# Where an expert's overflow block stands: in front of its products instead of between them

## The chip, the cores and the metric

The kernel runs on one core of a Trainium2 chip. Its engines work side by side and wait for one another through semaphores: PE (TensorE, the matrix products), DVE (VectorE), ACT (ScalarE), POOL (GpSimd), and SP (SyncE), which here issues all DMA transfers. The metric is the device time of one execution in microseconds; below, a time without another word is the median of the runs shown.

## What is computed

One layer of a diffusion backbone over 256 tokens of width 1024: a token mixer (Fourier mixing, a state space scan, gates and an output projection), and then a mixture of experts, 4 of 32 for each token. Only the last part is touched by the change, apart from some preparation for it. In the reference it is

```python
logits = (tok @ w_router + b_router).astype(jnp.float32)
top_logit, top_idx = lax.top_k(logits, TOP_K)
top_w = jax.nn.softmax(top_logit, axis=-1)
...
def expert_block(args):
    xe, e = args
    gu = xe @ w_gate_up[e] + b_gate_up[e]
    gate = jnp.minimum(gu[:, :D_FF], SWIGLU_LIMIT)
    up = jnp.clip(gu[:, D_FF:], -SWIGLU_LIMIT, SWIGLU_LIMIT)
    act = (up + 1.0) * gate * jax.nn.sigmoid(SWIGLU_ALPHA * gate)
    return act @ w_down[e] + b_down[e]
...
x = x + g2 * moe_ffn(h2, ...)
return rmsnorm(x, final_norm_w)
```

A token's four results are weighted with `top_w` and added up; `g2` is a row that depends on the conditioning vector. The weights of one expert are 12 MB in float32.

## The kernel before

**The weights.** `expert_chunk` loads an expert's weights in twelve copies of 1 MB (128 partitions of 2048 floats): numbers 0 to 7 are the rows of gate and up, 8 to 11 those of down. All copies of all experts, 384, go through SP's one queue in that order. They land in a ring of 19 tiles of 1 MB (`RING`); one of these holds router data at first, so that 18 copies are there before the first tile has to be used again. From then on a copy is issued when the tile of the copy 19 before it has been released, that is, when the last instruction that reads it is past. Copy 7 of expert e+1 takes the tile of copy 0 of expert e.

**One expert.** Each expert has 64 slots for tokens (`CAP`). For an expert `e` the loop at L1444 to L1493 writes, in the order of the program: the one-hot matrices for a later pair of experts, or in odd experts the weights for scattering (`weights_T`: four DVE instructions make `woh`, PE turns it over, ACT copies it to `woT`); `gate_up` (L1277, 64 products on copies 0 to 7, then four short products with `bgu` that add the bias); `gate_act` and `up_act` (DVE and ACT); `gather` (48 short products that fetch the tokens of a later pair into `xe`); in even experts `scatter_pair`, which adds the results of the pair before to `acc`; `act_T` (PE turns the activations, DVE copies them to `aT`); `overflow`; `down` (L1323, 32 products on copies 8 to 11); and `gated`, where DVE multiplies with `g2b`.

**The overflow block.** `overflow` is a branch on the number of the expert's tokens, which all engines take. Only where it is over 64 does `block32` run: it gathers 32 more tokens, makes their gate and up products from the same copies 0 to 7 (in two passes, on the banks `gu`), their down products from copies 8 to 11, and scatters them. With these inputs it runs in experts 9, 20 and 24, once each. Since the block may read copies 0 to 7, their tiles are released only when PE is past the branch. A hint for the branch's target (`mark_branch_hint_location`) is given to PE in the first products of `gate_up`.

**The order.** In this part the program's order is each engine's order (`manual_schedule`). Waits on what another engine made ahead of a branch are waits for that engine to be past the branch.

**The bias of down** is added for all experts at once, in expert 1 (`down_bias`, L1243): PE turns the routing weights, multiplies them with `b_down` (`bd`, held in `xe[1]`), and DVE multiplies with `g2r` and adds to `acc`. Since `bd` occupies `xe[1]`, both gathers of the second pair follow in expert 1.

**Ahead of the experts** `bias_parts` (L484) splits the gate and up biases into three bfloat16 parts in `bgu`, so that short products with a selecting matrix `sel` add them; it is called four times while the gates of the mixer are computed. `routing_weights` makes the softmax weights on DVE and ACT.

Of the kernel before, what the change touches and what calls it, by code (L numbers as in the profile page):

```python
# [22 lines left out]
NE = 32  # L23
# [38 lines left out]
def build(tc, A, out):  # L62
# [37 lines left out]
    bgu = const.tile([96, 2048], BF16, name="bgu")  # L100
    sel = const.tile([96, 32], BF16, name="sel")
# [384 lines left out]
    def bias_parts(q):  # L486
        b0, b1 = t2("bg", (96, 512)), t2("bgh", (96, 512), BF16)
        sl = slice(q * 512, (q + 1) * 512)
        for i in range(3):
            nc.sync.dma_start(b0[32 * i:32 * i + 32], A["b_gate_up"][0, :, sl])  # L490
        S.activation(b1, b0, AF.Copy)
        V.tensor_sub(b0, b0, b1)
        V.tensor_copy(bgu[0:32, sl], b1[0:32])
        V.tensor_copy(bgu[32:64, sl], b0[32:64])
        V.tensor_copy(b1[64:96], b0[64:96])
        V.tensor_sub(bgu[64:96, sl], b0[64:96], b1[64:96])
# [339 lines left out]
    for ch in range(2):  # L836
        for q in range(2):
            bias_parts(2 * ch + q)
# [152 lines left out]
    g2r = few[:, 0:1024]  # L991
# [7 lines left out]
    wT = few[0:32, 1024:1280].rearrange("p (t c) -> p t c", t=2)  # L999
# [5 lines left out]
    def ahead():  # L1005
# [12 lines left out]
        yield rows_bc(g2r, modd[3072:4096])  # L1018
# [107 lines left out]
    ohx = keepA.tile([128, 2, 64], BF16, name="ohx")  # L1126
    woh, woT = (keepA.tile([128, 2, 128], F32, name=n) for n in ("woh", "woT"))
# [50 lines left out]
    bd = xe[1][0:32].rearrange("p a b -> p (a b)")  # L1178
# [8 lines left out]
    def gather_tokens(ps, o, k, tb, start, stop, **kw):  # L1187
        for part in range(3):
            T.matmul(ps, h2p[tb][part][:, k * 128:(k + 1) * 128], o[:, tb, :], start=start and part == 0,
                     stop=stop and part == 2, **kw)  # L1190
# [12 lines left out]

    def first_gather(k4, tb):
        for k in range(4):
            gather_tokens(xp[k4][:, k, :], oh[0], k4 * 4 + k, tb, tb == 0 and k == 0, tb == 1,
                          skip_group_check=True)
# [35 lines left out]
    def down_bias():  # L1243

        tp = bank("t", 3, shape=(128, 2, 128))
        for tb in range(2):
            T.transpose(tp[0:32, tb, :], wn[:, tb, :], ident)
        V.tensor_copy(wT, tp[0:32])
        tmp = ga
        for tb in range(2):  # L1250
            for n in range(2):
                ps = bank("sc", 2)
                T.matmul(ps, wT[:, tb, :], bd[:, n * 512:(n + 1) * 512], start=True, stop=True)
# [295 lines left out]
```

## Time and profile before

| | us |
|---|---|
| time, median of 3 runs (1599.68 to 1601.88) | 1599.94 |
| the profiled execution | 1596.67 |
| its span, from the first to the last instruction | 1594.9 |
| first product of expert 0, after the span's start | 582.91 |
| PE busy | 1432.5 (90%) |
| DVE busy | 660.2 (41%) |
| moved by DMA | 511.75 MB |

The experts take the time from 583 us to the end. The profile cuts the span into 40 slices and gives the busy share of the engines, the granted clock of PE and the DMA rate in each. It groups the instructions by line, with their busy time and what they waited for; a timeline gives single instructions, with the time that their engine sat idle before them and, behind an arrow, what ended that idle time. `PEq L1425` as such an end means that PE's sequencer had got past the branch at L1425, `DVEq L1425` that DVE's had. PEld stands for PE's loading of weights, which goes on beside its products.

### The profile page before, as it was taken

The page shows a single profiled execution, that of the slowest core. Times are in us where ns is not written, and L with a number is a line of the kernel's source. Part 1 is how long each engine was busy: PE and PEld are TensorE (multiplying, and loading weights), DVE is VectorE, ACT ScalarE, POOL GpSimd, SP SyncE. Part 2 cuts the span into 40 slices and gives each one's busy share as a digit, 9 for nine tenths or more (in the row PEclk, how much of TensorE's full clock was granted, in tenths as well). Part 3 has the DMA queues.
Part 4 walks back from the last instruction along what each step waited for, and adds up shares of the span by engine and source line. Part 5 has one row for each costly group of instructions (what it writes and reads, how often), then busy time and mean ns, then how long its engine had stood idle before and what let it go on. Part 6 is the DMA issues. An engine that isn't in the chain of part 4 may idle for free. (4 is left out here: it accounts for less than half of the span.)

```text
span 1594.9 us, 21869 instructions
## 1 busy us (share of the span) xinstructions
PE 1432.5 (90%) x8684; PEld 806.0 (51%) x8684; DVE 660.2 (41%) x1158; ACT 304.1 (19%) x635; POOL 200.9 (13%) x165
## 2 busy tenths in 40 slices
PE   6998988889999988998988889989888989899897
PEld 4887766678899753433333333433334334343332
DVE  5776887885575743212222222212213123121222
ACT  3446354444555420000000000000000000000001
POOL 0155143332460410000000000000000000000000
PEclk8999999999999978999999999999989999999999
DMA  9625244578769757999999899999997999699993
GB/s 290 215 76 192 87 125 158 151 231 278 274 235 339 268 211 316 384 418 418 419 418 418 351 418 418 418 419 418 418 419 299 418 418 417 257 418 418 418 418 154
DMA packets 121636, 511.75 MB, mean 321 GB/s; under 512 B 13800, under 2 KB 30928, under 8 KB 72448
## 3 DMA queue, kind: packets, MB, share of 16 engines
q1 hardware_dynamic: 121472, 509.56, 81.8%
q8 instruction: 103, 1.69, 0.4%
q14 instruction: 61, 0.50, 0.1%
HBM read 508.33 MB, written 1.20 MB: 319 GB/s over the span
## 5 line engine op out<-in xcount | busy, mean ns | idle before, releaser
L1277 PE MATMUL ps_gu<-wexp,xe 128*64 128x512 f32 x2048 | 462.2, 607 | 6.3 <-DMA wexp<-in_w_gate_up 6.3
L1277 PEld LDWEIGHTS ps_gu<-wexp,xe 128*64 128x64 f32 x2048 | 157.1, 140 | 294.9 <-issue 269.9
L1323 PE MATMUL ps_dn<-wexp,aT 128*64 128x512 f32 x1024 | 234.2, 610 | 32.5 <-DVEq L1425 21.3
L1292 DVE TENSOR_SCALAR ga<-ps_gu 128x512 f32<-128x512 f32 x32 | 22.1, 691 | 437.7 <-issue 405.6
L1323 PEld LDWEIGHTS ps_dn<-wexp,aT 128*64 128x64 f32 x1024 | 85.6, 140 | 169.8 <-issue 120.3
L343 PE MATMUL ps_mm<-hh,wh 128*128 128x256 f32 (+1 forms) x496 | 166.8, 336 | 2.3 <-DVE cv L472 2.3
L345 PE MATMUL ps_mm<-hh,wl 128*128 128x256 f32 (+1 forms) x496 | 163.1, 329 | 0.0
L344 PE MATMUL ps_mm<-hl,wh 128*128 128x256 f32 (+1 forms) x496 | 162.6, 328 | 0.0
L1293 ACT ACTIVATE ga<-ga 128x512 f32<-128x512 f32 x32 | 20.2, 631 | 660.5 <-DVE ga L1292 660.5
L1328 DVE TENSOR_TENSOR yp<-ps_dn,g2b 64x512 f32<-64x512 f32 x60 | 41.3, 689 | 231.1 <-PE ps_dn L1323 230.6
L336 POOL TENSOR_TENSOR wl<-wraw,wh 128x512 fp32r<-128x512 f32 x78 | 105.0, 1349 | 218.7 <-ACT wh L333 164.0
L1502 POOL TENSOR_TENSOR ssq<-ssq,mhalf 128x1 f32<-128x1 f32 x2 | 1.1, 550 | 1013.2 <-DVE ssq L1501 1013.2
L343 PEld LDWEIGHTS ps_mm<-hh,wh 128*128 128x128 f32 x496 | 95.3, 192 | 23.8 <-issue 7.7
L345 PEld LDWEIGHTS ps_mm<-hh,wl 128*128 128x128 f32 x496 | 95.5, 193 | 10.0 <-issue 2.2
L344 PEld LDWEIGHTS ps_mm<-hl,wh 128*128 128x128 f32 x496 | 95.4, 192 | 8.2 <-issue 1.2
L333 ACT ACTIVATE wh<-wraw 128x512 fp32r<-128x512 f32 x132 | 81.1, 627 | 86.3 <-PE ps_mm L344 71.6
L472 DVE SCALAR_TENSOR_TENSOR cv<-ps_mm,par,cv 128x508 f32<-128x508 f32 (+3 forms) x116 | 80.8, 697 | 5.0 <-ACT cv L466 3.2
L336 DVE TENSOR_TENSOR wl<-wraw,wh 128x512 fp32r<-128x512 f32 x54 | 49.8, 924 | 36.3 <-ACT wh L333 35.5
L1334 DVE TENSOR_TENSOR acc<-acc,ps_sc 128x512 f32<-128x512 f32 x76 | 51.5, 685 | 19.0 <-PE ps_sc L1332 17.0
L1332 PE MATMUL ps_sc<-yp,woT 128*128 128x512 f32 x120 | 57.4, 601 | 0.0
L706 ACT ACTIVATE ab<-ab,nacs 128x128 f32<-128x128 f32 x128 | 42.1, 390 | 51.9 <-POOL ab L703 51.7
L1310 ACT ACTIVATE woT<-ps_t 128x256 f32<-128x256 f32 x15 | 5.8, 384 | 237.2 <-PE ps_t L1309 237.2
(373 smaller groups left out, 1809.5 us busy)
## 6 DMA issues: line engine op xcount, KB each, us to landing
wexp<-in_w_gate_up SPq DMA_DIRECT2D x256, 1024.0 KB, 19.9
wexp<-in_w_down SPq DMA_DIRECT2D x127, 1024.0 KB, 19.9
wraw<-in_w_in SPq DMA_DIRECT2D x32, 1024.0 KB, 5.0
wmod<-in_w_mod SPq DMA_DIRECT2D x64, 256.0 KB, 5.3
wmod<-in_w_mod SPq DMA_DIRECT2D x16, 512.0 KB, 8.3
ab<-ad SPq DMA_DIRECT2D x32, 256.0 KB, 3.7
eb<-ad SPq DMA_DIRECT2D x32, 256.0 KB
wssd<-in_w_ssd_out SPq DMA_DIRECT2D x8, 1024.0 KB, 8.6
```

The costliest lines, as they stand in the source:

```text
L333: S.activation(shp, w, AF.Copy)
L336: e.tensor_sub(low.rearrange("p (k n) -> p k n", n=128), w, shp.bitcast(F32))
L343: T.matmul(ps[:, :N], hi, hh[k][:, :N], start=k == 0 and start, stop=False, **kw)
L344: T.matmul(ps[:, :N], hi, hl[k][:, :N], start=False, stop=False, **kw)
L345: T.matmul(ps[:, :N], low, hh[k][:, :N], start=False, stop=k == 7, **kw)
L472: V.scalar_tensor_tensor(yv[:, :, a], pv[:, :, b], convw(k, blk), yv[:, :, a], op0=OP.mult, op1=OP.add)
L706: S.activation(ab[:, h, :], ab[:, h, :], AF.Exp, bias=nacs[:, c, j0 + h:j0 + h + 1])
L1277: mm = T.matmul(ps[half][h * 64:h * 64 + 64, :], x[:, k, :], w[k][:, half, h * 512:(h + 1) * 512], start=k == 0, stop=False)
L1323: T.matmul(pd[n * 64:n * 64 + 64, :], aT[:, j, h * 64:h * 64 + 64], w[8 + h * 2 + j // 2][:, j % 2, n * 512:(n + 1) * 512], start=i == 0, ...
L1328: V.tensor_mul(y, p[n * 64:n * 64 + 64, :], g2b[n * 64:n * 64 + 64])
L1332: T.matmul(p, lhsT, rhs, start=True, stop=True)
L1334: V.tensor_add(av, av, p)
```

## The change

`overflow(e, n_e, w)` is called ahead of the expert's `gate_up`. Its wide products use the banks `t` instead of `gu`. Outside the branch, copies 0 to 7 are now read last by `gate_up`. The hint moves: that for expert e+1 is given after the second wide product of `down` of expert e, and that for expert 0 in `first_gather`.

`down` begins with two short products that add the down bias from `bdn`, which two more calls of `bias_parts` make, scaled by 1.702; `down_bias`, `g2r`, `bd` and `wT` go, and with them the copy of `g2r` and that of `b_down` in float32. The gathers of the second pair are spread over experts 0 and 1 as for all others.

`weights_T` is parted: `weights_of` (DVE) stays ahead of `gate_up`, `weights_turned` (PE and ACT) goes behind `gather`. `act_T` writes its result over the expert's own tokens in `xe` instead of to `aT`.

```diff
     def bias_parts(q):
...
+        if q > 3:
+            sl, src, dst = slice((q - 4) * 512, (q - 3) * 512), A["b_down"], bdn
         for i in range(3):
-            nc.sync.dma_start(b0[32 * i:32 * i + 32], A["b_gate_up"][0, :, sl])
+            nc.sync.dma_start(b0[32 * i:32 * i + 32], src[0, :, sl])
+        if q > 3:
+            V.tensor_scalar_mul(b0, b0, ALPHA)
...
-        for q in range(2):
-            bias_parts(2 * ch + q)
+        for q in range(3):
+            bias_parts(3 * ch + q)
...
-    def down_bias():
...
+    def weights_turned(t):
         tp = bank("t", 3, shape=(128, 2, 128))
         for tb in range(2):
             T.transpose(tp[:, tb, :], woh[:, tb], ident)
         S.activation(t, tp, AF.Copy)
...
-    def down(w, aT):
+    def down(e, w, aT, hint=None):
         pd = bank("dn", 1)
+        for n in range(2):
+            T.matmul(pd[n * 64:n * 64 + 64, :], sel[:, e:e + 1].to_broadcast([96, 64]), bdn[:, half(n)],
+                     start=True, stop=False)
...
-        p = bank(*GU[0], shape=(128, 256))
+        p = bank("t", 3, shape=(128, 256))
...
+    def hint_after(mm, hint):
+        with tc.issue_after(mm.ins):
+            tc.mark_branch_hint_location(hint, "LikelyTaken", [ET.PE])
...
         n_e = nc.values_load(cnt[0:1, e:e + 1], min_val=0, max_val=256)
-
-        if e == NE - 2:
-            wo2 = [xe[1 - p2][:, 2 * i:2 * i + 2, :] for i in range(2)]
-            for i in range(2):
-                weights_T(wo2[i], first, (e + i,))
-        elif e % 2 and not last:
-            weights_T(woT, first, (e - 1, e))
-        elif e + 2 < NE:
+        overflow(e, n_e, w)
+
+        if e >= NE - 2:
+            wo2.append(xe[0][:, 2 * (e % 2):2 * (e % 2) + 2, :])
+            weights_of(first, (e,))
+        elif e % 2:
+            weights_of(first, (e - 1, e))
+        else:
             one_hot(oh[1 - p2], (e + 2, e + 3), 0)
-        pg, pu = gate_up(e, xs, w, last_between if last else None, f"spill{e}")
+        pg, pu = gate_up(e, xs, w, last_between if last else None)
         gate_act(pg)
         up_act(pu)
-        if last:
-            GU[0] = ("t", 3)
-        if e == 1:
-            down_bias()
-        if e > 1 and e // 2 * 2 + 2 < NE:
+        if e // 2 * 2 + 2 < NE:
             gather(xe[1 - p2], oh[1 - p2], e % 2)
+        if e >= NE - 2 or e % 2:
+            weights_turned(wo2[-1] if e >= NE - 2 else woT)
         if e and e % 2 == 0:
             scatter_pair(0)
-        act_T(aT)
+        act_T(xs)
         if e and e % 2 == 0:
             scatter_pair(1)
...
-        if e == 1:
-            for k4 in range(2):
-                gather(xe[1], oh[1], k4)
-        overflow(e, n_e, w)
-        pd = down(w, aT)
+        pd = down(e, w, xs, None if last else f"spill{e + 1}")
```

How this moves PE's instructions is seen at three places. The first is the end of the branch of expert 17 on PE, before the change. The unconditional branch closes the block, `ps_dn` are the products of `down`, `ps_gu` those of `gate_up` of expert 18, and a DMAHW is the landing of a copy:

```order
L1425 UNCONDITIONAL_BRANCH [waits PE_49]
L1323 MATMUL ps_dn<-wexp,aT 64x512 [waits DMAHW5_49,DVE_49,PE_49]
L1323 MATMUL ps_dn<-wexp,aT 64x512 x3
L1323 MATMUL ps_dn<-wexp,aT 64x512 [waits DMAHW6_49]
L1323 MATMUL ps_dn<-wexp,aT 64x512 x3
L1323 MATMUL ps_dn<-wexp,aT 64x512 [waits DMAHW7_49]
L1323 MATMUL ps_dn<-wexp,aT 64x512 x3
L1323 MATMUL ps_dn<-wexp,aT 64x512 [waits DMAHW0_49]
L1323 MATMUL ps_dn<-wexp,aT 64x512 x3
L1457 TENSOR_LOAD cnt
L1277 MATMUL ps_gu<-wexp,xe_6123 64x512 [waits DMAHW1_49]
L1277 MATMUL ps_gu<-wexp,xe_6123 64x512 x3
```

After the change the branch of expert 17 stands between the last products of expert 16's `down` (here L1326) and the first of `gate_up` of expert 17 (here L1274); the rows of the block itself are left out:

```order
L1326 MATMUL ps_dn<-wexp,xe_6143 64x512 [waits DMAHW0_49]
L1326 MATMUL ps_dn<-wexp,xe_6143 64x512 x3
L1463 TENSOR_LOAD cnt
L1431 COMPARE_AND_BRANCH
...
L1433 UNCONDITIONAL_BRANCH [waits PE_49]
L1431 UNCONDITIONAL_BRANCH [waits PE_49]
L1274 MATMUL ps_gu<-wexp,xe_6143 64x512 [waits DMAHW1_49,PE_49]
L1274 MATMUL ps_gu<-wexp,xe_6143 64x512
```

The first wide product behind the branch waited for DVE and waits now, in all experts but expert 0, for a copy and for PE's own work alone; the load of the count and the comparison now follow `down` directly.

The second place is the start of expert 0 on PE. Before, its first products follow the load of the count, and the branch comes later:

```order
L1457 TENSOR_LOAD cnt [waits DVE_49]
L1277 MATMUL ps_gu<-wexp,xe_6122 64x512 [waits DMAHW0_49,DVE_49]
L1277 MATMUL ps_gu<-wexp,xe_6122 64x512
L1277 MATMUL ps_gu<-wexp,xe_6122 64x512 [waits Activation_49]
L1277 MATMUL ps_gu<-wexp,xe_6122 64x512
```

After, they follow the branch, and wait for DVE, and from the third group on for ACT, behind it:

```order
L1431 UNCONDITIONAL_BRANCH [waits PE_49]
L1274 MATMUL ps_gu<-wexp,xe_6143 64x512 [waits DMAHW6_49,DVE_49]
L1274 MATMUL ps_gu<-wexp,xe_6143 64x512
L1274 MATMUL ps_gu<-wexp,xe_6143 64x512 [waits PE_49]
L1274 MATMUL ps_gu<-wexp,xe_6143 64x512
L1274 MATMUL ps_gu<-wexp,xe_6143 64x512 [waits DMAHW0_49]
L1274 MATMUL ps_gu<-wexp,xe_6143 64x512 x3
L1274 MATMUL ps_gu<-wexp,xe_6143 64x512 [waits DMAHW2_49,Activation_49]
```

On DVE and on ACT `routing_weights` stands ahead of this branch.

The third place is PE's order between `gather` and `down` in expert 17. Before (`ps_t` with `h2q` is the end of the gather, with `up` it is `act_T`):

```order
L1189 LDWEIGHTS h2q_6121
L1189 MATMUL ps_t<-oh_5939,h2q_6121 128x128
L1316 MATMUL ps_t<-ctab,up 128x128 [waits DVE_49]
L1316 MATMUL ps_t<-ctab,up 128x128 x3
L1425 COMPARE_AND_BRANCH
```

After (`woh` are the scatter weights being turned, `bdn` the bias of down):

```order
L1191 LDWEIGHTS h2q_6142
L1191 MATMUL ps_t<-oh_5963,h2q_6142 128x128
L1305 MATMUL ps_t<-ctab,woh 128x128 [waits DVE_49,PE_49,Activation_49]
L1305 MATMUL ps_t<-ctab,woh 128x128 [waits DVE_49]
L1316 MATMUL ps_t<-ctab,up 128x128 [waits DVE_49]
L1316 MATMUL ps_t<-ctab,up 128x128 x3
L1322 LDWEIGHTS sel
L1322 MATMUL ps_dn<-bdn,sel 64x512 [waits PE_49]
L1322 LDWEIGHTS sel
L1322 MATMUL ps_dn<-bdn,sel 64x512
L1326 MATMUL ps_dn<-wexp,xe_6143 64x512 [waits DMAHW1_49,DVE_49]
```

The turning came in from the expert's start, the bias products are new, and the branch is gone from here.

## Rows read from the trace of the kernel before

**Rows 1.** The page, section 2: DMA rate in 40 slices of 40 us.

```profile
GB/s 290 215 76 192 87 125 158 151 231 278 274 235 339 268 211 316 384 418 418 419 418 418 351 418 418 418 419 418 418 419 299 418 418 417 257 418 418 418 418 154
```

**Rows 2.** SP queue's waits, whole span: waited for, us in total, times, longest.

```profile
SPq L984 <- PEq L1425: 192.2, 23, 24.1
...
SPq L984 <- PEq L1427: 67.7, 3, 29.1
```

**Rows 3.** Stretches: PE, PEld, DVE, ACT, POOL busy; granted clock; DMA share; GB/s.

```profile
590.00:600.00 10.00, 7.94 (x41) 2.78 (x38) 1.98 (x3) 0.63 (x1) 0.00 (x0) 1.00 0.00 1
...
630.00:640.00 10.00, 9.51 (x59) 5.77 (x57) 7.28 (x11) 0.00 (x0) 0.00 (x0) 0.66 0.20 84
...
1360.00:1370.00 10.00, 6.80 (x44) 2.37 (x44) 3.58 (x9) 0.38 (x1) 0.00 (x0) 1.00 0.00 0
```

**Rows 4.** Timeline, expert 0: start, us, instruction, [idle before, what ended it].

```profile
582.91 9.46 PE L1277 MATMUL ps_gu<-wexp,xe 128*64 128x512 f32 x42
...
586.85 1.28 ACT L1434 ACT_TABLE_LOAD   x1
...
587.57 0.18 DVE L1241 TENSOR_SCALAR wsc<-few 128x32 f32<-128x32 f32 x1
...
600.43 0.81 SPq L984 DMA_DIRECT2D wexp<-in_w_gate_up  x2
```

**Rows 5.** Timeline, experts 2 and 3, a pair without a wait for copies.

```profile
647.28 13.07 PE L1277 MATMUL ps_gu<-wexp,xe 128*64 128x512 f32 x60
...
661.01 0.63 PE L1287 MATMUL ps_gu<-bgu,sel 96*64 96x512 bf16 x4
...
665.51 0.68 DVE L1317 COPY aT<-ps_t 128x512 f32<-128x512 f32 x1
...
667.94 7.09 PE L1323 MATMUL ps_dn<-wexp,aT 128*64 128x512 f32 x32 [0.88 <-DVEq L1425]
...
677.06 0.77 PE L1309 MATMUL ps_t<-ctab,woh 128*128 128x128 f32 x2 [2.03 <-DVE woh L1305]
677.76 13.96 PE L1277 MATMUL ps_gu<-wexp,xe 128*64 128x512 f32 x64
...
694.17 0.75 PE L1316 MATMUL ps_t<-ctab,up 128*128 128x128 f32 x4 [0.58 <-DVE up L1297]
...
695.81 7.09 PE L1323 MATMUL ps_dn<-wexp,aT 128*64 128x512 f32 x32 [0.89 <-DVEq L1425]
...
702.70 1.88 PE L1277 MATMUL ps_gu<-wexp,xe 128*64 128x512 f32 x7
```

**Rows 6.** Timeline, expert 24: bias products, the block's down products, its own.

```profile
1343.52 0.63 PE L1287 MATMUL ps_gu<-bgu,sel 96*64 96x512 bf16 x4
...
1362.29 3.64 PE L1405 MATMUL ps_dn<-wexp,aTx 128*32 128x512 f32 x32 [0.52 <-DVE aTx L1399]
...
1371.31 1.08 PE L1323 MATMUL ps_dn<-wexp,aT 128*64 128x512 f32 x4 [0.88 <-DVEq L1427]
```

**Rows 7.** Timeline: a copy's issue after a hole, and PE waiting for a later copy.

```profile
890.46 0.33 SPq L984 DMA_DIRECT2D wexp<-in_w_gate_up  x1
...
1141.42 1.94 PE L1277 MATMUL ps_gu<-wexp,xe 128*64 128x512 f32 x8 [0.56 <-DMA wexp<-in_w_gate_up]
```

**Rows 8.** PE's sequencer, lines L1457, L1425, L1427: ns min/median/max; then expert 31's branch.

```profile
L1457 PEldq TENSOR_LOAD <-cnt x32: 300/306/495, 580.9 to 1546.4; - x32
...
L1425 PEldq COMPARE_BRANCH  x32: 74/349/3862, 599.6 to 1574.3; - x32
...
L1427 PEldq COMPARE_BRANCH  x6: 195/264/344, 889.2 to 1370.6; - x6
...
1577.04 1.51 PE L1323 MATMUL ps_dn<-wexp,aT 128*64 128x512 f32 x6 [0.30 <-PEq L1425]
```

**Rows 9.** Stretch at the start of expert 5, columns as in rows 3.

```profile
730.00:740.00 10.00, 7.85 (x29) 2.44 (x28) 2.36 (x6) 0.38 (x1) 0.00 (x0) 0.83 1.02 418
```

**Rows 10.** Timeline: the first products of expert 31.

```profile
1550.65 1.92 PE L1277 MATMUL ps_gu<-wexp,xe 128*64 128x512 f32 x8
```

More of the change, by code (lines that the diff above doesn't have):

```diff
@@ L100, in build @@
     bgu = const.tile([96, 2048], BF16, name="bgu")
+    bdn = const.tile([96, 1024], BF16, name="bdn")
     sel = const.tile([96, 32], BF16, name="sel")
@@ L1188, in gather_tokens @@
         for part in range(3):
-            T.matmul(ps, h2p[tb][part][:, k * 128:(k + 1) * 128], o[:, tb, :], start=start and part == 0,
-                     stop=stop and part == 2, **kw)
+            mm = T.matmul(ps, h2p[tb][part][:, k * 128:(k + 1) * 128], o[:, tb, :], start=start and part == 0,
+                          stop=stop and part == 2, **kw)
+        return mm
     pk = bank("acc", 8, shape=(128, 4, 32))
@@ L1241, in routing_weights @@
             V.tensor_scalar_mul(wsc[:, tb, :], wn[:, tb, :], 1.0 / ALPHA)
-    def down_bias():
[L1245 to L1253, printed above, removed]
-                V.tensor_mul(tmp, ps, g2r[:, n * 512:(n + 1) * 512])
-                av = acc[:, tb, n * 512:(n + 1) * 512]
-                V.tensor_add(av, av, tmp)
-    ga, up, aT = wt("ga", (128, 512)), wt("up", (128, 512)), wt("aT", (128, 4, 128))
+    ga, up = wt("ga", (128, 512)), wt("up", (128, 512))
     xex = wt("xex", (128, 8, 64))
     ssq3 = keep.tile([128, 2, 4], F32, name="ssq3")
+    ohx = keep.tile([128, 2, 64], BF16, name="ohx")
+    woh, woT = (keep.tile([128, 2, 128], F32, name=n) for n in ("woh", "woT"))
     def gather(x, o, k4):
@@ L1269, in gather, with gate_up @@
         V.tensor_copy(x[:, k4 * 4:k4 * 4 + 4, :], ps)
-    def gate_up(e, x, w, between=None, hint=None):
-        ps = [bank(*GU[0]) for _ in range(2)]
+    def gate_up(e, x, w, between=None, tag=("gu", 2)):
+        ps = [bank(*tag) for _ in range(2)]
         for k in range(8):
@@ L1276, in gate_up @@
                 for h in range(2):
-                    mm = T.matmul(ps[half][h * 64:h * 64 + 64, :], x[:, k, :],
+                    T.matmul(ps[half][h * 64:h * 64 + 64, :], x[:, k, :],
                                   w[k][:, half, h * 512:(h + 1) * 512], start=k == 0, stop=False)
-            if hint and k == 0:
-                with tc.issue_after(mm.ins):
-                    tc.mark_branch_hint_location(hint, "LikelyTaken", [ET.PE])
             if between:
@@ L1400, in block32 @@
         pd = bank("dn", 1)
+        for n in range(2):
+            T.matmul(pd[n * 64:n * 64 + 32, :], sel[:, e:e + 1].to_broadcast([96, 32]), bdn[:, half(n)],
+                     start=True, stop=False, tile_position=(0, n * 64))
         for j in range(4):
@@ L1435, in build @@
     first = slots_of(0).unsqueeze(1).to_broadcast([128, 2, 64])
+    wo2 = []
     def last_between(k):
```

47 lines of the change are left out of this document (23 added, 24 removed).

## The prediction

> **What bounds the kernel now.** I read the DMA rate first. From 640 us on it stands at 418 GB/s in most slices, and that is the rate at which the experts' weights can come; so the end is set by the stream of 384 copies, by the holes in it, and by what PE does after the last copies. The holes are to be found in three ways. The slices show 351, 299 and 257 GB/s where experts 9, 20 and 24 are [rows 1]. Shorter stretches show a whole 10 us without a byte at 590 us and at 1360 us, and a share of 0.20 at 630 us [rows 3]. SP's waits say what ended them: PE's sequencer past L1425, 192.2 us in 23 waits, the longest 24.1, and past L1427, 67.7 us in the three experts with a block [rows 2]. So copies stand still because tiles aren't free, and tiles aren't free because PE isn't past a branch. PE itself is the faster of the two between the holes: an even expert takes 677.06 - 2.03 - 647.28 = 27.75 us, an odd one 702.70 - 677.76 = 24.9, with 2.8 between them for the wait of 2.03 us and the turning of the scatter weights; a pair makes 55.4 us [rows 5]. The copies of a pair, 24 times 1.0486 MB at 418 GB/s or 2.51 us, take 60.2.
>
> **The change part by part.** Its first effect is on tiles. Copies 0 to 7 are now read last by `gate_up`, so the first tile comes free after 8 of the 64 products (13.96 us [rows 5]), 1.75 us into an expert, instead of at the branch, 17 to 20 us into it. That gives the stream about seven copies' more room.
>
> *Start of the stage.* Expert 0 begins later than before, at 582.91 [rows 4], since its products now wait for DVE to be past the branch, and on DVE and ACT the routing weights come first. DVE ends them at 587.75, ACT its table load at 588.13 [rows 4]; a load of the count (0.306 on PE, the nearest row [rows 8]) leads to 588.3. That is a loss of 5.4 us for PE. The copies gain nevertheless: copy 18 can be issued at 588.3 + 1.75 = 590.1, where it was 600.43 [rows 4].
>
> *The stream.* From a restart to a landing I use one pair of rows: copy 127 (counted from 0) was issued at 890.46, and PE got copy 223 at 1141.42 [rows 7]. That is 251.0 us for 97 copies, or 97 x 2.51 = 243.5 and 7.5 for issue and landing. Now does a block in front make a hole? In expert 9 the block needs copy 119, which lands at 590.1 + 102 x 2.51 + 7.5 = 853.6. PE would be there earlier (588.3 plus nine experts of 26 us is some 825), so it waits for the copy. Behind the landing the block has half its down products left, 1.8 of 3.64 us, and then 5.4 us to its end [rows 6], say 7.2; the first tile is free 1.75 us later, at 862.6. The stream runs into the full ring after copy 126, at 590.1 + 109 x 2.51 = 863.7. So there is no hole to speak of. The same holds for expert 20: its last copy, 251, lands at 590.1 + 234 x 2.51 + 7.5 = 1184.9, and PE waits for it.
>
> *From there PE sets the end.* The block of expert 20 ends at 1184.9 + 7.2 = 1192. Behind it come:
> - expert 20's own work, an even expert: 27.75, less the wait of 0.88 for DVE to be past the branch (the copy that `down` needs had ended at 666.19, the wait at 667.94 [rows 5]), plus two bias products, half of the 0.6 us that four take [rows 5]: 27.2;
> - experts 21 to 30, five pairs of 24.9 + 27.2 = 52.1: 260.5. The wait of 2.03 us and the turning are gone from the odd experts' start; the turning fits into the 0.58 us in which PE waits for `up`, and in odd experts the bias products fit into the 0.89 us in which it waits for DVE's copy [rows 5]. If those covers were gone, 0.7 and 0.3 us for each would be back, 5 us in all;
> - the block of expert 24: from the bias products to `down` 27.8 us, where an undisturbed even expert takes 6.9, so 20.9 [rows 5, 6], and 1.5 more, since DVE, which must make the block's one-hot matrix, first multiplies the expert before (two instructions like the copy of 0.68 [rows 5]): 22.4;
> - expert 31 and the end, as before: 1594.9 - 1550.65 = 44.2 [rows 10].
>
> Together 1192 + 27.2 + 260.5 + 22.4 + 44.2 = 1546.3, without the branches and clock.
>
> *The branch in front.* This is the unknown. It was covered by DVE's work; now load and comparison stand between two runs of products, and PE has nothing else. Behind them on PE are all products of the expert, and all of DVE and ACT wait for these. The nearest row is expert 31's branch, where DVE had long been done: PE sat idle for 0.30 us [rows 8]; with a load of 0.306 us directly ahead I take b = 0.6. The lower end is 0.3, or nothing if the sequencer is far enough ahead. The upper end is the longest comparison, 3.862 against a median of 0.349 us [rows 8], or 3.5 us more. I stay near the low end because the median is that of a branch without such a delay, and because inner branches, which have no hint, took 0.195 to 0.344. There are 11 branches from expert 21 on: 6.6 us.
>
> *Clock.* At the start of expert 5 PE's granted clock falls to 0.83 over 10 us, so 3.4 us at the lower level, 1.2 GHz, and 1.7 us lost [rows 9]. This is the first of seven such openings among the 15 odd experts, all behind the wait of 2.03 us. With that wait gone I take two in the last five: 3.4 us; the ends are 0 and 8.
>
> *Ahead of the experts*, two more calls of `bias_parts`: six DVE instructions of 0.3 to 0.7 us for each, some 6.5 us, beside PE, which is busy there. I take 1 us for it; the ends are -1 (a 0.5 MB copy is gone) and 6. `down_bias` goes from expert 1, where the share of 0.20 was [rows 3]; its gain lies within the stream's path above.
>
> Sum: 1546.3 + 6.6 + 3.4 + 1 = 1557.3 against a span of 1594.9, so 37.6 us less. The median of the runs, 1599.94, lies 5.0 above that span (the profiled execution, 1596.67, 1.8 above); I put the same on top: **1562**.
>
> **The rivals.**
> - *Fetches come late now and then.* The hint is given some 6.5 us ahead of the branch, where `gate_up` and more, over 15 us, lay between. With half the branches 2.2 us late, b is 1.7, and the sum 1546.3 + 18.7 + 3.4 + 1 = 1569.4, or 1574. From b = 2.0 on PE bounds the whole stage: 588.3 + 24.9 + 15 x 52.1 + 3 x 22.4 + 44.2 = 1506.1, plus 31 b. At 2.4 with some clock losses that is 1587, or 1592.
> - *Every front branch pays for its fetch: slower.* The place is the same; the price is 3.5 us, the longest comparison less the median. Then 1506.1 + 31 x 3.5 + 1 = 1615.6, or 1621. It decides from b = 2.87, where that line reaches 1594.9. Against it speak the medians of both kinds of branch [rows 8]. The Trainium skill, page "Runtime: NRT & Kernel Launch", section "Instruction fetch mechanics", has this as a rule: a taken branch whose target is not in the pages at hand forces a fetch and a stall. By that rule the sum would be this rival's; the trace agrees in single cases alone, with 0.349 us at the median and 3.862 at the most [rows 8].
> - *It doesn't do what it says: the holes at the blocks stay*, because the block holds all twelve tiles while it waits for the down copies and the ring fills meanwhile. Then only the start (10.3 us) and expert 1 (8 us of the 10 at 630 [rows 3]) are won: 1576.6, or 1582. My times for expert 9, 862.6 against 863.7, leave little room, and a slower block would open the hole.
> - *Better than forecast:* no clock loss, b = 0.3 and nothing lost ahead: 1549.6, or 1555; this lies within the forecast's own range, 1552 to 1568.
>
> **How the numbers follow.** The forecast has 0.62, late fetches 0.17, the holes 0.10, the slower rival 0.06, and 0.05 is for times under 1548, with copies or pairs faster than my rows. The range goes from 1548 to 1588: it takes in the holes and most of the late fetches and leaves out the slower rival, the upper part of the late fetches and the low tail, some 0.15. A difference of 0.2% (3.2 us) is about what a measurement of this kernel can tell from none. Faster by more than that has 0.92 (the forecast, the low tail, the holes and nearly all of the late fetches), within it 0.02, slower 0.06.
>
> **What would show it.** In the profile after: the first product of expert 0 near 588.3 and the next copy's issue near 590; SP waiting on PE's products in place of its branches; 418 GB/s in all slices from 600 us to 1300 us, with PE waiting for copies ahead of expert 9 and 20; an idle time of about 0.6 us before the first product of each expert; no wait for `woh`, and 52 us a pair in experts 21 to 30. Wrong would be a first product of each expert that comes 2 us or more after `down`, comparisons with a median over 1 us, copies that stand still for over 5 us in expert 9 or 20, or products of `gate_up` that wait for DVE.

## The result, and the profile after

The changed kernel takes 1578.09 us (1576.80 to 1580.02, four runs) against 1600.04 us of the kernel before: a ratio of 0.9862, with a 95% interval of 0.9844 to 0.9879. The profiled execution has a span of 1575.2 us, 19.7 less than before. The forecast was 1562 us, a span of 1557.3. The direction and the range were right; the gain is 22 us where 38 were expected, and the missing 17.9 us of span are the subject of what follows.

In the changed kernel the three nested branches are L1431, L1433 and L1435 (L1425, L1427, L1429 before), the gate and up products L1274, the down products L1326, the copies of the experts' weights L991. The DMA rate in 40 slices of 39.4 us, from the page:

```profile
GB/s 280 232 64 208 85 130 160 121 218 280 248 192 354 256 216 417 418 416 418 418 416 419 359 417 418 416 419 416 419 417 403 419 416 402 303 419 416 417 418 136
```

Beside [rows 1], the slice of expert 20 has risen from 299 to 403, that of expert 24 from 257 to 303, that of expert 9 hardly (351, 359). Ahead of the experts, slices 11 and 12 (394 to 473 us) are lower than before, 248 and 192 for 274 and 235.

The SP queue's waits (us in total, times, longest), the rows that answer to [rows 2]:

```profile
SPq L991 <- PE ps_gu L1274: 152.5, 92, 22.0
...
SPq L991 <- PE ps_acc L1067: 22.0, 1, 22.0
...
SPq L991 <- PEq L1431: 13.5, 11, 1.4
```

SP waits for products now, and no longer for branches: 13.5 us in place of 192.2. The move does what it says. The waits for the blocks' own branch (67.7 before) have become waits for the first products behind a block, the longest 22.0 us at expert 24. The second row, also 22.0 us, is another thing: it is the eighth copy of expert 0, which waits for products ahead of the experts (see x4).

Expert 0 and the start of experts 1 to 3, from PE's timeline (start, us, instruction, in brackets the idle time before and what ended it):

```profile
592.03 2.68 PE L1191 MATMUL ps_acc<-oh,h2q 128*128 128x128 bf16 x24
597.99 2.83 PE L1274 MATMUL ps_gu<-wexp,xe 128*64 128x512 f32 x6 [3.27 <-DVE few L1249]
...
625.02 13.95 PE L1274 MATMUL ps_gu<-wexp,xe 128*64 128x512 f32 x64 [0.31 <-PEq L1431]
...
642.11 0.41 PE L1322 MATMUL ps_dn<-bdn,sel 96*64 96x512 bf16 x2
642.96 7.09 PE L1326 MATMUL ps_dn<-wexp,xe 128*64 128x512 f32 x32 [0.45 <-DVE xe L1317]
650.36 13.95 PE L1274 MATMUL ps_gu<-wexp,xe 128*64 128x512 f32 x64 [0.31 <-PEq L1431]
...
677.52 2.79 PE L1274 MATMUL ps_gu<-wexp,xe 128*64 128x512 f32 x12 [0.16 <-PEq L1431]
```

Expert 1 to expert 3 is 677.52 - 625.02 = 52.5 us, where [rows 5] had 55.4. The wait for `woh` is gone; the two bias products take 0.41. Expert 0, though, begins at 597.99 and not at 588.3.

Behind the blocks of experts 9, 20 and 24, and PE's wait for copy 247, the last gate copy of expert 20 (the same view):

```profile
876.67 3.68 PE L1274 MATMUL ps_gu<-wexp,xe 128*64 128x512 f32 x8 [5.48 <-PEq L1433]
...
1192.83 1.08 PE L1379 MATMUL ps_t<-wexp,xex 128*32 128x256 f32 x8 [1.41 <-DMA wexp<-in_w_gate_up]
...
1211.41 1.94 PE L1274 MATMUL ps_gu<-wexp,xe 128*64 128x512 f32 x8 [0.56 <-PEq L1433]
...
1343.78 8.72 PE L1274 MATMUL ps_gu<-wexp,xe 128*64 128x512 f32 x28 [5.64 <-PEq L1433]
```

By the prediction copy 247 lands at 590.1 + 230 x 2.51 + 7.5 = 1174.9; it came at 1192.83, 17.9 us later. That is the whole of the miss: from the end of expert 20's block to the end of the span are 1575.2 - 1211.41 = 363.8 us, and the forecast had 1557.3 - 1192 = 365.3. In between, expert 20's block waited for copy 247 and not, as the prediction had it, for 251, and ended 18.6 us after it where the forecast had 17.1; the two differences of 1.5 us cancel. So the question is why the copies are late by then. Two places offer themselves: expert 0's late start, and the 5.5 us of idle PE behind the blocks.

PE's sequencer at the first two branches (ns min/median/max):

```profile
L1431 PEldq COMPARE_BRANCH  x32: 74/2324/4383, 593.3 to 1526.4; - x32
...
L1433 PEldq COMPARE_BRANCH  x6: 207/378/6068, 870.1 to 1343.3; - x6
```

The comparison in front lasts 2.3 us at the median (0.349 in [rows 8]), and still PE sits idle for 0.31 us only: the sequencer reaches it while products are queued. The second branch, which every block passes, has 6.068 us at the most, where [rows 8] had 0.344.

### The profile page after: what moved, and what is told of

Same layout as the page of the kernel before. It is cut to its first block, busy times and chain, and to the rows that moved or that the text cites. A ratio compares the mean times of both kernels' runs of the same rounds, so it can differ in the third digit from the quotient of the medians.

```text
span 1575.2 us, 22112 instructions
## 1 busy us (share of the span) xinstructions
PE 1436.9 (91%) x8744; PEld 803.6 (51%) x8744; DVE 655.5 (42%) x1161; ACT 305.1 (19%) x637; POOL 200.7 (13%) x165
## 5 line engine op out<-in xcount | busy, mean ns | idle before, releaser
L1274 PE MATMUL ps_gu<-wexp,xe 128*64 128x512 f32 x2048 | 457.7, 601 | 33.3 <-PEq L1433 11.7
L1274 PEld LDWEIGHTS ps_gu<-wexp,xe 128*64 128x64 f32 x2048 | 168.5, 138 | 321.0 <-issue 240.9
L1326 PE MATMUL ps_dn<-wexp,xe 128*64 128x512 f32 x1024 | 225.9, 594 | 7.2 <-DVE xe L1317 7.2
L1326 PEld LDWEIGHTS ps_dn<-wexp,xe 128*64 128x64 f32 x1024 | 71.1, 137 | 141.9 <-issue 125.9
L337 DVE TENSOR_TENSOR wl<-wraw,wh 128x512 fp32r<-128x512 f32 x54 | 45.1, 837 | 36.7 <-ACT wh L334 36.1
L1379 PE MATMUL ps_t<-wexp,xex 128*32 128x256 f32 x384 | 32.5, 481 | 13.5 <-DMA wexp<-in_w_gate_up 13.5
```

The costliest lines, as they stand in the source:

```text
L337: e.tensor_sub(low.rearrange("p (k n) -> p k n", n=128), w, shp.bitcast(F32))
L1274: T.matmul(ps[half][h * 64:h * 64 + 64, :], x[:, k, :], w[k][:, half, h * 512:(h + 1) * 512], start=k == 0, stop=False)
L1326: mm = T.matmul(pd[n * 64:n * 64 + 64, :], aT[:, 2 * j + h, :], w[8 + h * 2 + j // 2][:, j % 2, n * 512:(n + 1) * 512], start=False, stop= ...
```

## Where the front of the program loses 10 us

Followed by their order, PE's products are 1.4 us later than before at 421 us, 11.9 later at 467, and 11.8 still at 551. The other traces agree: between the same two products the seven kernels with the preparation in this place (the changed one, x2 to x4 and x6 to x8 below) lose 10.5 to 10.6 us, and the five without it (x1, x5, x9 to x11) lose nothing. In that stretch products of the gates alternate with the modulation's products, whose weights (`wmod`) come in copies of 256 KB. SP's issues in the two kernels, before and after:

```profile
389.95 6.36 SPq L223 DMA_DIRECT2D wmod<-in_w_mod  x7
403.42 1.12 SPq L243 DMA_DIRECT2D modd<-modrow  x4
404.64 0.54 SPq L232 DMA_DIRECT2D modrow<-in_b_mod  x1
```

```profile
392.42 1.30 SPq L224 DMA_DIRECT2D wmod<-in_w_mod  x3
393.81 3.25 SPq L495 DMA_DIRECT2D bg<-in_b_down  x3
404.24 0.81 SPq L244 DMA_DIRECT2D modd<-modrow  x3
405.09 1.24 SPq L495 DMA_DIRECT2D bg<-in_b_down  x3
406.38 0.28 SPq L244 DMA_DIRECT2D modd<-modrow  x1
406.70 1.77 SPq L224 DMA_DIRECT2D wmod<-in_w_mod  x4
412.19 0.54 SPq L233 DMA_DIRECT2D modrow<-in_b_mod  x1
```

Before the wait for `modrow` (until 403.4) seven `wmod` copies were issued; now three, and the four behind b_down's copies come after it. From then on PE gets its modulation weights piecemeal, and as each copy waits for the tile that PE frees, the lead never comes back (PE's timeline; before, and after):

```profile
420.12 1.06 PE L235 MATMUL ps_st<-wmod,csil 128*32 128x512 f32 x8
```

```profile
422.50 1.05 PE L236 MATMUL ps_st<-wmod,csil 128*32 128x512 f32 x4
424.38 1.04 PE L236 MATMUL ps_st<-wmod,csil 128*32 128x512 f32 x2
426.38 1.04 PE L236 MATMUL ps_st<-wmod,csil 128*32 128x512 f32 x2
```

PE counts as busy all through this stretch, and no idle row names a wait; only the starts of equal products, set side by side, show it.

## The experiments

All are edits of the changed kernel unless they say otherwise. Times are medians; the ratio is to the kernel before. Copy 247 is the time at which PE got it (no wait for it in x7 and x8, which is a dash).

| run | span | time | ratio, 95% | expert 0 | copy 247 |
|---|---|---|---|---|---|
| changed kernel | 1575.2 | 1578.1 | 0.9862, 0.9844 to 0.9879 | 597.99 | 1192.83 |
| x1_bias_later | 1571.8 | 1576.8 | 0.9843, 0.9815 to 0.9871 | 594.61 | 1190.32 |
| x2_inner_hint | 1570.6 | 1572.0 | 0.9806, 0.9775 to 0.9837 | 598.61 | 1193.34 |
| x3_weights_behind | 1583.1 | 1585.1 | 0.9895, 0.9868 to 0.9923 | 595.61 | 1202.48 |
| x4_ring_shift | 1573.0 | 1574.3 | 0.9829, 0.9797 to 0.9861 | 595.11 | 1191.31 |
| x5_bias_in_experts | 1565.0 | 1568.0 | 0.9797, 0.9759 to 0.9835 | 587.46 | 1185.26 |
| x6_early_hint | 1581.1 | 1583.5 | 0.9890, 0.9851 to 0.9929 | 599.82 | 1195.06 |
| x7_no_hint | 1644.1 | 1646.3 | 1.0284, 1.0235 to 1.0334 | 600.27 | - |
| x8_block_behind | 1596.0 | 1598.2 | 0.9988, 0.9970 to 1.0007 | 595.00 | - |
| x9_bias_and_hint | 1566.9 | 1565.6 | 0.9767, 0.9746 to 0.9788 | 593.35 | 1190.04 |
| x10_and_ring | 1558.7 | 1560.5 | 0.9728, 0.9705 to 0.9751 | 586.38 | 1181.69 |
| x11_and_first_hint | 1555.9 | 1559.2 | 0.9739, 0.9718 to 0.9760 | 583.53 | 1179.42 |

**x1, the preparation of b_down moved to the output products.**

```diff
-        for q in range(3):
-            bias_parts(3 * ch + q)
+        for q in range(2):
+            bias_parts(2 * ch + q)
...
         if kb == 2:
             norm_gate()
+        if kb in (3, 5):
+            bias_parts(4 + (kb == 5))
```

> One edit on the changed kernel (1578.1 us, span 1575.2): the two extra preparations (b_down) leave the stage of the gates' products and come in the middle of the Fourier output products. Theory A, the slip: in the changed kernel the products of w_mod arrive four, two and two, some 1.9 us apart, from 422 us on, since their copies are issued behind six more copies and a later write of the modulation row, and the front of the program ends 10 to 12 us late. Then here expert 0's first product goes from 597.99 to 586 to 588 us, expert 20's last gate copy (waited for at 1192.83) lands at 1181 to 1183, and the time falls by 9 to 12 us, to 1566 to 1569. Theory B, the slip comes from the shift of buffers (bdn in front of all others) and not from the place of the preparation: expert 0 stays at 597 to 599 and the time at 1576 to 1580. Theory C, the slip is real but the stream of copies hides it: expert 0 goes earlier by 10, the time by less than 3.

The gates' stage was cured: at 461 us PE is 1.4 us earlier than before, not 11.9 later. But expert 0 came only 3.4 us earlier, and the time 1.3. At 502 us PE was 3.3 later again, at 518 8.4. SP's waits from 455 to 520 us say why:

```profile
SPq L1013 <- DVE bdn L503: 20.7, 1, 20.7
```

L1013 is the load of `xr`, into a tile that takes over the memory in which b_down was split; it waited for the last reader, and the output projection's weights stood behind it in the queue. So the cause is right, but none of the three theories had this outcome: the same work in another place found another queue.

**x5, the preparation in the experts' stage,** with one pass on ScalarE and GpSimd in `xe`'s second buffer, which nobody uses yet.

```diff
+    bd = xe[1][0:96].rearrange("p a b -> p (a b)")
+    def down_parts():
+        S.activation(bdn, bd, AF.Copy, scale=ALPHA)
+        S.activation(bd, bd, AF.Copy, scale=ALPHA)
+        G.tensor_sub(bd, bd, bdn)
+        for g in (1, 2):
+            S.activation(bdn[32 * g:32 * g + 32], bd[32 * g:32 * g + 32], AF.Copy)
+        G.tensor_sub(bdn[64:96], bd[64:96], bdn[64:96])
...
                 expert_chunk(e + 1, i)
+                if e == 0 and i == 0:
+                    for g in range(3):
+                        nc.sync.dma_start(bd[32 * g:32 * g + 32], A["b_down"][0])
```

> One edit on the changed kernel (ratio 0.9862 to the kernel before, 1578.1 us): b_down is prepared in the stage of the experts, on ScalarE and GpSimd, in xe's second buffer, and leaves the gates' stage and its copies as they were before the change. Moving the preparation only to the output products cured the gates' stage (461 us: 1.4 us earlier than before instead of 11.9 later) but gave 9.8 us back at 488 to 502, since a later load (xr) took over the buffer that held b_down and waited 20.7 us for its last reader. Theory A (the slip is the preparation's, wherever its buffers and copies stand in the way): now expert 0 starts at 585 to 589 us, expert 20's last gate copy (1192.83) lands at 1181 to 1184, the ratio is 0.977 to 0.981 (1563 to 1570 us). Theory B (a front that is done earlier only lengthens the wait for the ring's buffers, the DMA hole at 556 to 574): expert 0 earlier by 10, the landing by less than 3, the ratio 0.984 to 0.987.

Theory A, though copy 247 came 1.3 us after its band. PE's timeline of this kernel, a modulation step, expert 0, copy 247 and the end of expert 24's block:

```profile
421.33 1.06 PE L236 MATMUL ps_st<-wmod,csil 128*32 128x512 f32 x8
```

```profile
587.46 2.83 PE L1274 MATMUL ps_gu<-wexp,xe 128*64 128x512 f32 x6 [3.31 <-DVE few L1249]
...
1185.26 1.08 PE L1379 MATMUL ps_t<-wexp,xex 128*32 128x256 f32 x8 [1.41 <-DMA wexp<-in_w_gate_up]
...
1334.28 15.96 PE L1274 MATMUL ps_gu<-wexp,xe 128*64 128x512 f32 x64 [3.51 <-PEq L1433]
```

The eight products of a step stand together again, expert 0 starts 10.5 us earlier, copy 247 comes 7.6 earlier, and the span falls by 10.2 (the median time by 10.1). Not all of the 10.2 is the preparation's: 7.6 are there at copy 247, and of the 2.6 behind it 2.1 are expert 24's jump, which took 3.51 us for 5.64 and lies between 2.84 and 4.04 in x1, x3, x4 and x6. So the preparation that the prediction priced at 1 us cost 10.5 at expert 0 and 7.6 to 10 at the end.

**x2, a hint inside the block for the branch behind it.**

```diff
-            with tc.If(n_e > CAP + 32):
+            with tc.If(n_e > CAP + 32, label=f"more{e}"):
...
         for k4 in range(2):
-            gather(x, o, k4)
+            mm = gather(x, o, k4)
+        if i == 0:
+            hint_after(mm, f"more{e}")
```

> One edit on the changed kernel (1578.1 us, span 1575.2): the branch behind a first overflow block gets a prefetch hint of its own, after the block's token products. Theory A: the 5.48 us of idle PE behind expert 9's block and the 5.64 behind expert 24's are the late fetch of that branch's target; they fall under 0.6 each; the DMA hole behind expert 9 (0.72 and 0.84 at 870 to 890) shrinks by 4 to 5, and the time falls by 8 to 11 us, to 1567 to 1570. Theory B: the wait is a cost of running into a block behind a branch that was announced as taken (what was fetched was the wrong side), which a second hint doesn't cure: 5 to 6 us of idle stay at both, the time stays at 1576 to 1580.

PE's sequencer at this branch, and the first product behind expert 9's block:

```profile
L1436 PEldq COMPARE_BRANCH  x6: 197/276/357, 871.8 to 1341.4; - x6
```

```profile
873.50 7.07 PE L1275 MATMUL ps_gu<-wexp,xe 128*64 128x512 f32 x24 [0.56 <-PEq L1436]
```

The late fetch is cured as theory A had it, 6.068 us to 0.357 at the most. The gain is half of what it expected, 4.6 us of span; by the ratios it is 9 us with some 6 either way, so it is the traces that decide. Expert 24's part arrives in full. What is won at expert 9 (its down products begin 3.7 us earlier) is still there at the down products of expert 16 (1078.4 for 1082.0) and gone at those of expert 17 (1106.7 for 1106.6), whose gate products now wait for copies; expert 18 waits for a copy that lands no earlier (1122.54 for 1122.02). So the hole at expert 9 was not on the path of the copies. Why not, although more was moved by 900 us, the runs don't show.

The copies lose time elsewhere. PE gets copy 99, in expert 8, at 814.74 in the changed kernel and at 815.48 here:

```profile
814.74 1.94 PE L1274 MATMUL ps_gu<-wexp,xe 128*64 128x512 f32 x8 [1.18 <-DMA wexp<-in_w_gate_up]
```

```profile
815.48 1.94 PE L1275 MATMUL ps_gu<-wexp,xe 128*64 128x512 f32 x8 [0.17 <-DMA wexp<-in_w_gate_up]
```

From there to copy 247 are 378.1 and 377.9 us, and 377.8 to 379.5 in x1, x3 to x6 and x9 to x11, with the hole at expert 9 or without it. The prediction's 148 x 2.51 makes 371.5. So 6.6 of the 17.9 us are lost in this stretch, and 6 to 8 us in each of the other kernels too. What takes them isn't shown.

**x6, the outer hint earlier.** It is marked behind the first gate products of the expert before instead of its first down products.

```diff
+            if hint and k == 0:
+                hint_after(mm, hint)
...
-        pd = down(e, w, xs, None if last else f"spill{e + 1}")
+        pd = down(e, w, xs)
```

> One edit on the changed kernel (ratio 0.9862 to the kernel before, 1578.1 us): the prefetch hint for the next expert's branch stands behind the first gate products of the expert before instead of behind its first down products, some 17 us earlier. Theory A (the distance decides, for both branches, since both jump to the same place): PE's comparisons at the branch fall from a median of 2.3 us to under 0.5, the idle PE behind the blocks of experts 9 and 24 (5.48 and 5.64 us) falls under 1, the ratio is 0.979 to 0.982. Theory B (what the block itself runs through displaces what was fetched, so that only a hint inside the block helps): the comparisons get shorter, the 0.31 us at each branch stay or fall to 0.1, but the 5.5 us at experts 9 and 24 stay; the ratio is 0.984 to 0.987.

Theory B, for both branches: the comparison's median fell to 0.347 us, the 0.31 us of idle PE stayed, and so did the 5.5 behind expert 9's block:

```profile
L1433 PEldq COMPARE_BRANCH  x32: 74/347/4259, 595.2 to 1532.3; - x32
```

```profile
879.03 3.68 PE L1274 MATMUL ps_gu<-wexp,xe 128*64 128x512 f32 x8 [5.57 <-PEq L1435]
```

The 0.31 us thus doesn't hang on the length of the comparison. That the time rose by 5 us was not expected by either theory. In the profiled execution 0.8 of it are there by expert 20 (1212.20 for 1211.41), and 4.8 more come in expert 24's block (1349.39 for 1343.78). There PE sat idle amid the block's token products, with nothing that the profile names as the cause, while the jump behind the block cost 2.84 us in place of 5.64:

```profile
1325.21 0.21 PE L1191 MATMUL ps_t<-ohx,h2p 128*128 128x32 bf16 x1 [5.05 <-issue]
...
1349.39 16.59 PE L1274 MATMUL ps_gu<-wexp,xe 128*64 128x512 f32 x64 [2.84 <-PEq L1435]
```

From 1320 to 1330 us, around these 5.05 us, the granted clock was 0.53, near the lower level of 1.2 GHz (1.00 in the changed kernel, which has no such idle time). Whether the earlier hint brings this idle time or it came by chance, one trace can't say; all four runs of x6 lie above those of the changed kernel (1580.27 to 1584.98).

**x7, no hints.** All hints are left out (`hint_after` does nothing).

> One edit on the changed kernel (ratio 0.9862, 1578.1 us): no prefetch hints. Theory A (each jump over the block then pays a fetch, as the prediction's second rival had it at 3.5 us an expert, and as the 5.5 us behind the blocks suggest): 3 to 5.5 us of idle PE at each of the 29 jumps; up to expert 20 the copies hide about half of that; 40 to 60 us more, 1615 to 1640. Theory B (the comparisons last 2.3 us in the median even with a hint and are hidden behind queued products, so a longer one is hidden too): under 1 us each, 1575 to 1590.

Theory A, somewhat above its range: 68 us more. PE's waits in this kernel (us in total, times, longest):

```profile
PE ps_gu L1273 <- PEq L1430: 64.8, 26, 5.1
PE ps_gu L1273 <- issue: 19.2, 5, 8.3
PE ps_gu L1273 <- PEq L1432: 11.5, 3, 5.4
```

At 2.5 us a branch, what the prediction's slower rival feared is real, if smaller than its 3.5, and the hints in the changed kernel are what holds it off. By the rival's own sum 2.5 us would give 1584.6, and the span is 1644.1, so the 64.8 us are not all: PE also waited 19.2 us in five waits for which the profile names no cause, and what else made the kernel longer wasn't followed. The rule of the Trainium skill, page "Runtime: NRT & Kernel Launch", section "Instruction fetch mechanics", that a taken branch to a page not at hand stalls for its fetch, agrees with these rows. With a hint the same branch costs 0.31 us here.

**x3, expert 0's block behind its gate and up products.**

```diff
-        overflow(e, n_e, w)
+        if e:
+            overflow(e, n_e, w)
...
         pg, pu = gate_up(e, xs, w, last_between if last else None)
+        if e == 0:
+            overflow(e, n_e, w)
```

> One edit on the changed kernel (1578.1 us, span 1575.2): expert 0's branch and overflow block come behind its products of gate and up, so that they no longer wait for the routing weights on VectorE. Theory A (the prediction's step 1 as it was put: 5.4 us on the path): expert 0's first product goes from 597.99 to 592 to 594 us, and copies, which wait for its buffers, go on earlier; the time falls by 4 to 5.5 us, to 1573 to 1574. Theory B: the copies do not wait for it, since the DMA engines stand at 1.01 from 575 to 870 us without a gap, and the copies bound the program up to expert 20: expert 0 goes earlier by 5, the landing of expert 20's last gate copy (1192.83) and the time by less than 1.

Neither: expert 0's first product came earlier and waited for nothing, and the kernel became 7 us slower. Stretches of this kernel (columns as in [rows 3]) and SP's wait:

```profile
600.00:610.00 10.00, 10.00 (x50) 3.22 (x46) 1.16 (x6) 0.82 (x1) 0.00 (x0) 1.00 0.37 147
610.00:620.00 10.00, 8.64 (x60) 4.11 (x62) 3.27 (x5) 0.63 (x1) 0.00 (x0) 1.00 0.85 342
```

```profile
SPq L991 <- PEq L1431: 16.7, 1, 16.7
```

Expert 0's tiles come free behind its branch again, one wait of 16.7 us, and the DMA engines lose 6.3 + 1.5 = 7.8 us, the 7.9 by which the span grew. I had overlooked it when I wrote the theories. As it is, the run prices the change's own mechanism for a single expert.

**x8, the move alone undone.** The call of `overflow` stands ahead of `down` again; all else stays.

```diff
-        overflow(e, n_e, w)
...
+        overflow(e, n_e, w)
         pd = down(e, w, xs, None if last else f"spill{e + 1}")
```

> One part of the change undone: the branch and the overflow block stand behind the expert's activations again, ahead of its down products, as in the kernel before; the bias products, their preparation, the banks and the turning in the gap stay changed. Theory A (the gain is that of the move, and the bias preparation cost 10 to 12 us of it): the SyncE queue waits for PE's branches again and the hole at expert 0 is back; the time is that of the kernel before plus the slip less the turning and the second gather taken off the path, ratio 0.998 to 1.008. Theory B (the gain is that of the gap, the copy waits and the bias): ratio 0.985 to 0.992.

Theory A: 0.9988. SP's waits for PE's branches are back:

```profile
SPq L991 <- PEq L1431: 106.9, 19, 19.9
SPq L991 <- PEq L1433: 69.5, 3, 25.1
```

The move is worth 1596.0 - 1575.2 = 20.8 us, about all that the change gains. Not all of it need be the move's, though: the hint for an expert stays in the `down` of the one before, most of an expert ahead of the branch, and in the blocks of experts 9, 20 and 24 PE sits idle for 2.8, 2.8 and 3.5 us with no named cause, which no block of the kernel before has. Without these 9.1 us the move would still be worth 11.7. The rest of the change (bias products, turning in the gap, other banks) nets nothing, since it pays some 12 us in front: expert 0 begins at 595.00 here, at 582.91 in [rows 4].

**x4, 256 bytes of filler.** The tiles that left `keepA` had shifted the ring's upper buffers by 256 bytes, and the eighth copy of expert 0 then waited 22.0 us for products that read the memory below. `PAD = 80` becomes `PAD = 144`.

> One edit on the changed kernel (1578.1 us, span 1575.2): 256 bytes more of filler in front of the ring's upper buffers, which puts them where they were in the kernel before (the moved tiles had shifted them by 256 bytes). In the changed kernel the eighth copy of expert 0 waits 22.0 us for a product of L1067, and the DMA engines stand still from 556 to 574; in the kernel before they did not there. Theory A: that hole goes, the ring is full at about 584 to 590 us, a new hole waits for expert 0's products until 599 to 601, and the copies end up 2 to 3 us earlier: 1575 to 1576. Theory B: the hole in front and the slip of the preparation are one and the same loss: the time falls by 10 or more, to 1568 or less. Theory C: filled earlier and held up later by the same amount: within 1 us of 1578.

Theory A, at its small end: copy 247 is 1.5 us earlier, the span 2.2. (The times alone, whose intervals overlap, would not tell this from theory C.) From 560 to 570 us the DMA engines, which moved nothing there in the changed kernel, have a share of 0.49, and the hole has come back at 590, where the full ring waits for expert 0:

```profile
560.00:570.00 10.00, 9.44 (x40) 7.17 (x40) 7.95 (x12) 3.74 (x9) 3.96 (x4) 1.00 0.49 182
...
590.00:600.00 10.00, 9.51 (x62) 6.23 (x64) 2.83 (x16) 3.98 (x6) 0.00 (x0) 0.73 0.22 90
```

**x9 to x11, together:** x5 with x2, then with the filler of x4, then with expert 0's hint behind the first group of token products (`if tb == 0 and k4 == 0` for `if tb and k4 == 0`).

> The edits of x5 (b_down prepared in the stage of the experts) and of x2 (a hint inside the block for the inner branch) together. Theory A (the two losses are separate and add, and make up nearly all that the prediction missed, its span being 1557.3): span 1575.2 less 10.2 (x5) less 4.6 (x2) = 1560.4, ratio 0.972 to 0.978. Theory B (they overlap, since either only moves the copies up to expert 20): as the better of the two, span 1564 to 1566, ratio 0.979 to 0.981.

> x9 with the 256 bytes of filler of x4. Theory A (the DMA hole ahead of expert 0 is in part a loss, as in x4, whose span fell by 2.2): 1 to 3 us under x9, ratio 0.970 to 0.977. Theory B (the copies then wait for expert 0's products instead, one hole for the other): within 1 us of x9.

> x10 with the hint for expert 0's branch 18 groups of token products earlier, behind the first of them instead of behind the third. Theory A (expert 0's first product waits 3.3 us in the changed kernel not for the routing weights but for PE's own comparison, 4.4 us long and begun at 593.3, which fetches late; and the ring is full by then, so that its start is on the path of the copies): the comparison at expert 0 falls under 1 us, its first product comes 2 to 3.5 us earlier, and the time falls by 2 to 3.5 us against x10. Theory B (its start is not on the path, since the DMA engines are busy): its first product comes earlier, the time stays within 1 us of x10.

x9 lies between its theories: its ratio of 0.9767 is in theory A's band, with the upper end of the interval just outside it, but its span (1566.9) is no better than x5's. Its profiled execution was 5 us later than the kernel before at 340 us and 7.0 at 365, and no later from there to 570; what delays the front differs by some us from one execution to the next, and this one can't settle it. x10 is better than x9 by 0.4%, as x4 is better than the changed kernel by 0.3%; of the 8.2 us between their spans some 4 are x9's late front. x11 and x10 can't be told apart in time. But x11 settles what expert 0 waits for. PE's first product, and VectorE at that time:

```profile
583.53 2.80 PE L1275 MATMUL ps_gu<-wexp,xe 128*64 128x512 f32 x12 [0.30 <-PEq L1434]
```

```profile
586.49 0.18 DVE L1250 TENSOR_SCALAR wsc<-few 128x32 f32<-128x32 f32 x1
```

It starts 2.96 us before VectorE writes the first routing weights, and so doesn't wait for them. In x4 and x10 it starts ahead of them too, by 2.8 and 2.4 us.

x10 and x11, at 1560 us, are 1.1 to 1.4% faster than the changed kernel, and 2.6 to 2.7% faster than the kernel before.

## Why the prediction was right, and where it was short

- **What the move does: right.** SP's waits for branches fell from 192.2 to 13.5 us, and x3, for one expert, and x8 show that the move carries the gain, or most of it.
- **Ahead of the experts, 1 us with ends of -1 and 6: the step that failed.** The prediction counted the twelve DVE instructions of the two calls beside a busy PE. It did not count their six DMAs on SP, behind which four `wmod` copies are queued. Expert 0 begins 10.5 us later for it and copy 247 comes 7.6 us later (x5); that is 7.6 of the miss of 17.9 us. x1 and x5 move the DMAs and the instructions together, so that it is the DMAs is read from the order of SP's issues. Nor does the delay reach the copies as the prediction had it, from a full ring through expert 0's products: the ring isn't full, since the eighth copy, held by products ahead of the experts, is issued only at 572.86 (562.20 in x5).
- **A copy in 2.51 us: too small behind copy 99.** The 148 copies up to 247 take 378.1 us for 371.5, 6.6 us more, and much the same in every kernel that can be read so. This is the second large part of the miss, and its cause is open.
- **Expert 0, 5.4 us for the routing weights: size near, mechanism wrong.** With the preparation out of the way expert 0 began at 587.46, 4.6 us after [rows 4]. But x11 starts at 583.53, ahead of the weights. The 3.3 us belonged to PE's comparison, 4.4 us long and begun at 593.3; the profile put the wait down to VectorE because that ended last before it. Nor was it on the path of the changed kernel: there the DMA engines are busy from 575 to 870 us (416 to 419 GB/s in slices 16 to 22), and x11's earlier start is not seen in the time.
- **No hole in expert 9: wrong, but of little weight.** The first product behind the block came at 876.67, not at 853.6 + 7.2 = 860.8: the copies were 11.3 us late by expert 8 (copy 99 at 814.74 against 590.1 + 82 x 2.51 + 7.5 = 803.4), and 5.48 us went to the late branch. The engines lost 4.4 us from 870 to 890, but x2 shows that copy 247 owes nothing to it.
- **The block's inner branch: not seen.** "Inner branches, which have no hint, took 0.195 to 0.344" was read from a kernel with the block behind. With it in front two of three cost 5.5 us. (In x1 and x3 to x6, too, expert 9's cost 5.4 to 5.6, but expert 24's 2.8 to 4.0 and expert 20's 0.57 at the most.) x2 gives back 4.6 us of span.
- **b = 0.6: too large.** 0.31 at nearly all branches, 3.2 us less over 11. Clock at odd experts' starts: no drop; 3.4 us less. These two gains paid for expert 24's late branch (5.6) and the lower clock behind it, 0.56 from 1340 to 1350. So the tail fits to 1.5 us, by two errors that cancel.
- **Pairs of 52.1 us and 2b: right,** 52.5 between experts 1 and 3, and so were the last 44.2 (1575.2 - 1530.72 = 44.5).
- **Markers.** "Comparisons with a median over 1 us" would have called the forecast wrong: they were 2.3 us, and cost 0.31. A comparison's length says nothing while products are queued; PE's idle time does.

x5 gives 10.2 us and x2 4.6; together with the filler and the first hint the span is 1555.9 (1557.4 at the median of five executions), and the forecast had 1557.3. That is in part luck: copy 247 still comes 4.5 us after the forecast's 1174.9, and what follows it is 5.9 us shorter. The forecast's time can be had, but not from this change alone.

Open: why the inner branch's comparison is short when the block stands behind (0.436 us at the most in x8) and costs up to 5.6 us in front, since x6 shows that the hint's distance isn't it; what the idle times without a named cause are, inside the blocks of x8 and in x6 and x7; what takes the 6.6 us between copies 99 and 247; and what delays the front by some us in single executions.

## What to carry to other kernels

A step that is moved or added on a vector engine brings its DMAs with it: look at what is queued behind them, and at whose memory its tiles take, before calling it hidden. Where PE is busy all through a stretch, compare when equal products start, since a ring that has lost its lead shows no idle row. Where a rarely run block moves to another place, give every jump in it a hint, and price it by PE's idle time, not by the length of the comparison.

## What the runs showed of the hardware

- A jump over a block that the PE skips costs 0.31 us with a hint and 2.5 us without one (x7, 64.8 us in 26); a hint 17 us earlier (x6) shortens the comparison from 2.3 to 0.35 us, and the idle time not at all.
- A jump out of a block that has run, without a hint of its own, cost 5.4 to 5.6 us in expert 9, 2.8 to 5.6 in expert 24 and 0.57 at the most in expert 20, in six kernels; with one it cost 0.55 or 0.56 in all three (x2).
- 256 bytes in where a ring begins decide whether its eighth copy waits 22 us for another tile's readers (x4).
- PE can count as busy without a gap while it loses 10.5 us in some 40 to copies that come piecemeal (the gates' stage).
